# A 3x3 convolution: nine clipped taps in place of row pairs with a shared middle row

## The chip, the cores and the metric

The kernel runs on one core of a Trainium2 chip. The metric is the time of one execution on the device in microseconds; lower is better. Three runs of the kernel before took 132.85, 133.58 and 134.07 us, a median of 133.58.

## The reference

A 3x3 convolution with zero padding of one pixel, 16 images of 64 channels and 64x64 pixels, 128 output channels, all in f32:

```python
x:      (16, 64, 64, 64)   f32
weight: (128, 64, 3, 3)    f32
x_pad = np.pad(x, ((0, 0), (0, 0), (1, 1), (1, 1)), mode='constant')
for b, co, ci, kh, kw:
    output[b, co] += weight[co, ci, kh, kw] * x_pad[b, ci, kh:kh+h, kw:kw+w]
```

The output is (16, 128, 64, 64) in f32, 33.55 MB; the input x is 16.78 MB.

## The kernel before

**Loading.** Two images make a pair `p` (8 pairs): the 64 channels of one lie on partitions 0 to 63, those of the other on 64 to 127. Each pair has its own tile `xs` of 128 x 64 x 64 in f16, resident for the whole kernel. GpSimd's queue issues the loads (line 48), which cast f32 to f16 on the way: four pieces for pair 0 (rows 0-17, 18-31, 32-47, 48-63) and two for each other pair, eighteen in all, at the head of the program. The first piece holds every row that block 0 reads. SyncE's queue loads the weights (line 41) and later issues the stores.

**Weights.** ScalarE and VectorE cast the raw weights to f16, one kernel row `kh` at a time, and write each tap's 64 channels twice side by side (`w16`, lines 66 and 68). Nine transposes on TensorE (line 80) put them, channels on partitions, into PSUM, and as each was doubled the taps lie on both halves of the partitions. From PSUM five weight rows of three taps each are made in `Wt` (lines 86 to 90): G0, G1, G2 are the kernel's rows 0, 1, 2; G21 is row 2 minus row 1, G01 is row 0 minus row 1.

**The shared middle row.** Output rows are made in pairs 2j and 2j+1. With s[j] = x[2j] + x[2j+1], and U the convolution of s with the middle kernel row G1,

- output row 2j is U + G21 on x[2j+1] + G0 on x[2j-1],
- output row 2j+1 is U + G01 on x[2j] + G2 on x[2j+2].

That is five kernel rows of three taps for two output rows, where the direct form has six. The sums `ss` come from line 100: on VectorE in four pieces for pair 0, on GpSimd in two pieces for each other pair (one tile per pair, three tiles in rotation), kept in program order, so that GpSimd runs them behind the loads that it has to issue.

**Blocks.** Each pair has four blocks of 16 output rows (8 row pairs). A block has three groups of matmuls (line 137): U with 3 taps on `ss`; A with 6 taps for the even rows; B with 6 taps for the odd rows. A group has one PSUM tile of 128 x 8 x 64 for each of the two images. For a tap the two images' matmuls follow each other: one uses partitions 0 to 63 of weights and pixels, the other 64 to 127, so both halves of the array's rows are in use at once. Taps at the left and right column (kw 0 and 2) run over 63 columns, at the upper and lower image edge over 7 rows: no padded copy exists. A block is 3 x 2 + 6 x 2 + 6 x 2 = 30 matmuls of up to 512 columns.

**Evacuation.** ScalarE copies U's two tiles to SBUF (`ut`, line 151); VectorE adds A and U into the even rows of an output tile `ot` (line 156), B and U into its odd rows (line 159); SyncE stores each image's 16 rows, 512 KB (line 160). PSUM has eight tiles in rotation, `ot` sixteen, `ut` four. Waits between engines and the rotation of tiles are set by the framework from the program's order.

Of the kernel before, what the change touches and what calls it, by code (L numbers as in the profile page):

```python
# [8 lines left out]
F32 = mybir.dt.float32  # L9
F16 = mybir.dt.float16  # L10


@with_exitstack
def kernel(
    ctx: ExitStack,
    tc: tile.TileContext,
    x: bass.AP,
    weight: bass.AP,
    out: bass.AP,
):  # L20
    nc = tc.nc
    B, CI, H, W = x.shape
    CO = weight.shape[0]
    assert H == 64 and W == 64 and CI == 64 and CO == 128 and B % 2 == 0
    NP = B // 2
    RB = 8

    x_rows = x.rearrange("b c h w -> (b c) h w")
    out_rows = out.rearrange("b co h w -> b co h w")
    w_flat = weight.rearrange("co ci kh kw -> co (ci kh kw)")  # L30

    const = ctx.enter_context(tc.tile_pool(name="const", bufs=1))
    psum = ctx.enter_context(tc.tile_pool(name="psum", bufs=8, space=bass.MemoryType.PSUM))
    xpool = ctx.enter_context(tc.tile_pool(name="xpool", bufs=1))
    opool = ctx.enter_context(tc.tile_pool(name="opool", bufs=16))
    spool = ctx.enter_context(tc.tile_pool(name="spool", bufs=3))
    upool = ctx.enter_context(tc.tile_pool(name="upool", bufs=4))


    w_raw = const.tile([CO, CI, 9], F32)  # L40
    nc.sync.dma_start(w_raw.rearrange("p c t -> p (c t)"), w_flat)
    xs = []
    ident = const.tile([128, 128], F16)
    for p in range(NP):
        xt = xpool.tile([128, H, W], F16, tag=f"xs{p}", name="xs")
        cuts = [0, 18, 32, 48, 64] if p == 0 else [0, 32, 64]
        for lo, hi in zip(cuts[:-1], cuts[1:]):
            nc.gpsimd.dma_start(  # L48
                xt[:, lo:hi, :], x_rows[128 * p : 128 * p + 128, lo:hi, :]
            )  # L50
            if p == 0 and lo == 0:
                make_identity(nc, ident)
        xs.append(xt)


    w16 = const.tile([CO, 9, 2, CI], F16)
    for kh in range(3):
        src = (
            w_raw[:, :, 3 * kh : 3 * kh + 3]
            .rearrange("p c t -> p t c")  # L60
            .unsqueeze(2)
            .to_broadcast([CO, 3, 2, CI])
        )
        dst = w16[:, 3 * kh : 3 * kh + 3, :, :]
        if kh == 1:
            nc.vector.tensor_copy(dst, src)  # L66
        else:
            nc.scalar.copy(dst, src)  # L68

    Wt = const.tile([128, 5, 3, CO], F16)  # L70
    G0, G21, G1, G01, G2 = range(5)

    def wrow(i):
        return Wt[:, i, :, :].rearrange("p t c -> p (t c)")

    wps = {}
    for kh in (1, 0, 2):
        wp = psum.tile([128, 512], F32, tag="acc", name="wp")
        for k in range(3):
            nc.tensor.matmul(  # L80
                wp[:, k * CO : k * CO + CO],
                w16[:, 3 * kh + k, :, :].rearrange("p d c -> p (d c)"),
                ident,
            )
        wps[kh] = wp[:, 0 : 3 * CO]
    nc.vector.tensor_copy(wrow(G1), wps[1])  # L86
    nc.scalar.copy(wrow(G0), wps[0])  # L87
    nc.vector.tensor_sub(wrow(G21), wps[2], wrow(G1))  # L88
    nc.vector.tensor_sub(wrow(G01), wps[0], wrow(G1))  # L89
    nc.scalar.copy(wrow(G2), wps[2])  # L90


    ss = []
    for p in range(NP):
        st = spool.tile([128, H // 2, W], F16, tag="ss", name="ss")
        v = xs[p].rearrange("p (j i) c -> p j i c", i=2)
        step = 8 if p == 0 else 16
        for lo in range(0, H // 2, step):
            eng = nc.vector if p == 0 else nc.gpsimd
            add = eng.tensor_add(  # L100
                st[:, lo : lo + step, :], v[:, lo : lo + step, 0, :], v[:, lo : lo + step, 1, :]
            )
            if p > 0:
                tc.keep_in_program_order(add)
        ss.append(st)

        for blk in range(4):
            j0 = blk * RB

            def group(wi_rows):  # L110

                tiles = [
                    psum.tile([128, RB, W], F32, tag="acc", name="acc") for _ in range(2)
                ]
                n = 3 * len(wi_rows)
                i = 0
                for wi, off in wi_rows:
                    for kw in (1, 0, 2):
                        c_lo, c_hi = max(0, 1 - kw), min(W, W + 1 - kw)
                        for b2 in range(2):  # L120
                            p0 = 64 * b2
                            lo, hi = j0, j0 + RB
                            if off is None:
                                rhs = ss[p][p0 : p0 + 64, lo:hi, c_lo + kw - 1 : c_hi + kw - 1]
                            else:
                                while 2 * lo + off < 0:
                                    lo += 1
                                while 2 * (hi - 1) + off > H - 1:
                                    hi -= 1
                                first = 2 * lo + off  # L130
                                last = 2 * (hi - 1) + off
                                rhs = xs[p][
                                    p0 : p0 + 64,
                                    first : last + 1 : 2,
                                    c_lo + kw - 1 : c_hi + kw - 1,
                                ]
                            nc.tensor.matmul(  # L137
                                tiles[b2][:, lo - j0 : hi - j0, c_lo:c_hi],
                                Wt[p0 : p0 + 64, wi, kw, :],
                                rhs,  # L140
                                start=i == 0,
                                stop=i == n - 1,
                            )
                        i += 1
                return tiles

            U = group([(G1, None)])
            us = []
            for b2 in range(2):
                ut = upool.tile([128, RB, W], F32, tag="ut", name="ut")  # L150
                nc.scalar.copy(ut, U[b2])  # L151
                us.append(ut)
            ots = [opool.tile([128, RB, 2, W], F32, tag="ot", name="ot") for _ in range(2)]
            A = group([(G21, 1), (G0, -1)])
            for b2 in range(2):
                nc.vector.tensor_add(ots[b2][:, :, 0, :], A[b2], us[b2])  # L156
            Bt = group([(G01, 0), (G2, 2)])
            for b2 in range(2):
                nc.vector.tensor_add(ots[b2][:, :, 1, :], Bt[b2], us[b2])  # L159
                nc.sync.dma_start(  # L160
                    out_rows[2 * p + b2, :, blk * 16 : blk * 16 + 16, :],
                    ots[b2].rearrange("p j i c -> p (j i) c"),
                )


# [28 lines left out]
```

## Time and profile before

| | |
|---|---|
| median of three runs | 133.58 us |
| the profiled execution | 133.58 us, its span 131.8 us |
| TensorE matmul / weight load busy | 109.0 us (83%) / 53.5 us |
| VectorE busy | 84.5 us (64%) |
| ScalarE busy | 38.2 us (29%) |
| GpSimd busy | 39.6 us (30%) |
| mean granted TensorE clock | 0.956 |
| loads (software queue) | 8.39 MB written, 32.8% of the DMA engines' span |
| stores and weights (hardware queue) | 33.85 MB, 64.4% |
| HBM | 17.07 MB read, 33.55 MB written |

The span runs from the first to the last instruction of the profiled execution; the time of the execution has a little around it. A matmul's busy time is pipelined: neighbours overlap, so the sum of durations exceeds the busy time, and the pace has to be read from the starts. In a line of the groups stand the source line, the engine, the operation, what is written from what, the shapes and count; behind the first bar the busy time in us and the mean of one in ns; behind the second the engine's idle time just before them and what ended it. A line of the timeline has start and duration in us, engine, operation and how many are merged in it; in brackets the idle time before and its releaser.

### The profile page before, as it was taken

To read this page: it belongs to the slowest core of one execution; us is meant where nothing else is said; L and a number is where in the kernel's file an instruction comes from. 1 tells how busy PE (TensorE), PEld (TensorE's weight loads), DVE (VectorE), ACT (ScalarE), POOL (GpSimd) and SP (SyncE) were. 2 spreads that over 40 slices of the span, in tenths; PEclk is the share of its full clock that TensorE was granted. 3 is DMA by queue.
4 is the path that set the end of the run, shared out by engine and by line. 5 is a ranking of instruction groups with operands and counts; after the bars stand their busy time and mean duration, and the time that the engine had idled before them with its cause. 6 is when DMAs were issued, how large, how long until landed. Compare 5 with 4: busy or idle time off the path is not lost.

```text
span 131.8 us, 2482 instructions
## 1 busy us (share of the span) xinstructions
PE 109.0 (83%) x969; PEld 53.5 (41%) x969; DVE 84.5 (64%) x136; ACT 38.2 (29%) x69; POOL 39.6 (30%) x38
## 2 busy tenths in 40 slices
PE   0329999400899999999999999999999999999910
PEld 0203444200344555445554545554455544555400
DVE  0263777700057778777877777777778777877750
ACT  3604233000303333333333333333333333333300
POOL 6832131016999293009201910290000000000000
PEclk9999999975579999999999999999999999999997
DMA  3899999999999999999999999999999999888884
GB/s 97 115 185 208 211 216 280 285 280 277 277 277 271 277 278 285 276 302 411 421 420 419 410 418 418 419 415 416 418 419 411 421 404 369 348 351 332 334 332 159
DMA packets 11963, 42.39 MB, mean 322 GB/s; under 512 B 1328, under 2 KB 1456, under 8 KB 11952
## 3 DMA queue, kind: packets, MB, share of 16 engines
q1 hardware_dynamic: 9360, 33.85, 64.4%
q0 software_dynamic: 2592, 8.39, 32.8%
q8 instruction: 7, 0.11, 0.3%
q14 instruction: 4, 0.03, 0.1%
HBM read 17.07 MB, written 33.55 MB: 384 GB/s over the span
## 4 chain that ended last, share of the span: by engine, by line
PE 66%; DMA 21%; issue 4%; POOL 2%; DVE 1%; ACTq 1%; DVEq 0%; ACT 0%; POOLq 0%
PE acc L137 66%; DMA xs<-in_x_dram 21%; POOL ss L100 2%; ACTq L189 1%; DVE ot L156 1%; POOL xs L48 0%; DVEq L189 0%; DVE ot L159 0%; POOL ident masks.py:197 0%; ACT ut L151 0%; POOLq L178 0%
## 5 line engine op out<-in xcount | busy, mean ns | idle before, releaser
L137 PE MATMUL acc<-xs,Wt 64*128 64x504 f16 (+3 forms) x768 | 90.9, 385 | 0.0
L137 PEld LDWEIGHTS <-Wt 64*128 64x128 f16 x960 | 52.7, 97 | 66.9 <-issue 14.6
L156 DVE TENSOR_TENSOR ot<-acc,ut 128x512 f32<-128x512 f32 x64 | 41.2, 686 | 33.5 <-PE acc L137 17.1
L151 ACT COPY ut<-acc 128x512 f32<-128x512 f32 x64 | 34.4, 589 | 79.6 <-issue 75.3
L159 DVE TENSOR_TENSOR ot<-acc,ut 128x512 f32<-128x512 f32 x64 | 41.2, 685 | 1.1 <-PE acc L137 1.1
L100 POOL TENSOR_TENSOR ss<-xs 128x1024 f16<-128x1024 f16 x14 | 29.3, 2121 | 28.4 <-issue 28.4
L137 PE MATMUL acc<-ss,Wt 64*128 64x504 f16 (+1 forms) x192 | 27.6, 392 | 12.1 <-POOL ss L100 8.8
L48 POOL DMA_DIRECT2D xs<-in_x_dram x18 | 9.7, 547 | 20.7 <-DMA xs<-in_x_dram 19.9
L80 PE MATMUL wp<-ident,w 128*128 128x128 f16 x9 | 1.3, 306 | 4.5 <-DVE w L66 4.5
L100 DVE TENSOR_TENSOR ss<-xs 128x512 f16<-128x512 f16 x4 | 1.7, 423 | 4.1 <-DMA xs<-in_x_dram 4.1
L66 DVE CAST w<-w_raw 128x384 f16<-128x384 f32 x1 | 0.8, 836 | 3.6 <-DMA w_raw<-in_weight_dram 3.6
L80 PEld LDWEIGHTS <-w 128*128 128x128 f16 x9 | 0.8, 132 | 4.8 <-DVE w L66 4.5
L68 ACT CAST w<-w_raw 128x384 f16<-128x384 f32 x2 | 1.7, 873 | 1.6 <-DMA w_raw<-in_weight_dram 1.6
L90 ACT CAST Wt<-wp 128x384 f16<-128x384 f32 x1 | 0.5, 478 | 3.9 <-DVE Wt L88 3.9
L68 ACT ACT_TABLE_LOAD x1 | 1.3, 1283 | 0.7 <-PEq L178 0.7
L88 DVE TENSOR_TENSOR Wt<-wp,Wt 128x384 f16<-128x384 f32 x1 | 0.6, 559 | 0.1
L86 DVE CAST Wt<-wp 128x384 f16<-128x384 f32 x1 | 0.6, 551 | 0.0
L89 DVE TENSOR_TENSOR Wt<-wp,Wt 128x384 f16<-128x384 f32 x1 | 0.5, 548 | 0.0
L87 ACT CAST Wt<-wp 128x384 f16<-128x384 f32 x1 | 0.5, 478 | 0.1
masks.py:199 POOL TENSOR_SCALAR_AFFINE_SELECT ident<-ident 128x128 f16<-128x128 f16 x1 | 0.3, 304 | 0.1
masks.py:197 POOL MEMSET ident<- 128x128 f16 x1 | 0.2, 223 | 0.0
L178 POOL MEMSET const-float32-0.0<- 128x1 f32 x1 | 0.1, 98 | 0.2 <-issue 0.2
(3 smaller groups left out, 0.3 us busy)
## 6 DMA issues: line engine op xcount, KB each, us to landing
out_dram<-ot SPq DMA_DIRECT2D x64, 512.0 KB, 10.1
xs<-in_x_dram POOLq DMA_DIRECT2D x14, 512.0 KB, 25.5
xs<-in_x_dram POOLq DMA_DIRECT2D x2, 256.0 KB, 7.2
w_raw<-in_weight_dram SPq DMA_DIRECT2D x1, 288.0 KB, 2.9
xs<-in_x_dram POOLq DMA_DIRECT2D x1, 288.0 KB, 5.7
xs<-in_x_dram POOLq DMA_DIRECT2D x1, 224.0 KB, 6.1
```

The lines of the kernel that those rows point to most:

```text
L48: nc.gpsimd.dma_start(xt[:, lo:hi, :], x_rows[128 * p : 128 * p + 128, lo:hi, :])
L66: nc.vector.tensor_copy(dst, src)
L68: nc.scalar.copy(dst, src)
L80: nc.tensor.matmul(wp[:, k * CO : k * CO + CO], w16[:, 3 * kh + k, :, :].rearrange("p d c -> p (d c)"), ident,)
L86: nc.vector.tensor_copy(wrow(G1), wps[1])
L88: nc.vector.tensor_sub(wrow(G21), wps[2], wrow(G1))
L100: add = eng.tensor_add(st[:, lo : lo + step, :], v[:, lo : lo + step, 0, :], v[:, lo : lo + step, 1, :])
L137: nc.tensor.matmul(tiles[b2][:, lo - j0 : hi - j0, c_lo:c_hi], Wt[p0 : p0 + 64, wi, kw, :], rhs, start=i == 0, stop=i == n - 1,)
L151: nc.scalar.copy(ut, U[b2])
L156: nc.vector.tensor_add(ots[b2][:, :, 0, :], A[b2], us[b2])
L159: nc.vector.tensor_add(ots[b2][:, :, 1, :], Bt[b2], us[b2])
L189: with _tile.TileContext(nc) as tc:
```

## The change

The row sums, the five weight rows and the combination behind PSUM go. The nine taps' weights are copied from PSUM as they are (`Wt` of nine taps, three per copy, the middle row on VectorE, the others on ScalarE). A block of 16 output rows has four PSUM tiles: two halves of 8 rows for each of two images. For each of nine taps it has four matmuls, the halves outside and the images inside, and each reads the resident pixels directly, clipped to rows and columns that exist. Two tiles are copied to `ot` by VectorE (first image), two by ScalarE (second image), and SyncE stores 512 KB for each image as before. The loads (line 48), the casts and the transposes are not touched; the tiles `ss` and `ut` are no longer there.

```diff
-    spool = ctx.enter_context(tc.tile_pool(name="spool", bufs=3))
-    upool = ctx.enter_context(tc.tile_pool(name="upool", bufs=4))
...
-    Wt = const.tile([128, 5, 3, CO], F16)
...
+    Wt = const.tile([128, 9, CO], F16)
     for kh in (1, 0, 2):
         wp = psum.tile([128, 512], F32, tag="acc", name="wp")
...
-        wps[kh] = wp[:, 0 : 3 * CO]
-    nc.vector.tensor_copy(wrow(G1), wps[1])
-    nc.scalar.copy(wrow(G0), wps[0])
-    nc.vector.tensor_sub(wrow(G21), wps[2], wrow(G1))
-    nc.vector.tensor_sub(wrow(G01), wps[0], wrow(G1))
-    nc.scalar.copy(wrow(G2), wps[2])
+        dst = Wt[:, 3 * kh : 3 * kh + 3, :].rearrange("p t c -> p (t c)")
+        if kh == 1:
+            nc.vector.tensor_copy(dst, wp[:, 0 : 3 * CO])
+        else:
+            nc.scalar.copy(dst, wp[:, 0 : 3 * CO])
...
-            add = eng.tensor_add(
-                st[:, lo : lo + step, :], v[:, lo : lo + step, 0, :], v[:, lo : lo + step, 1, :]
-            )
...
-            U = group([(G1, None)])
...
-                nc.scalar.copy(ut, U[b2])
...
-            A = group([(G21, 1), (G0, -1)])
...
-                nc.vector.tensor_add(ots[b2][:, :, 0, :], A[b2], us[b2])
-            Bt = group([(G01, 0), (G2, 2)])
...
-                nc.vector.tensor_add(ots[b2][:, :, 1, :], Bt[b2], us[b2])
...
+    taps = [(1, 1), (1, 0), (1, 2), (0, 1), (0, 0), (0, 2), (2, 1), (2, 0), (2, 2)]
     for p in range(NP):
...
         for blk in range(4):
...
+            pst = [
+                psum.tile([128, RB, W], F32, tag="acc", name="acc") for _ in range(4)
+            ]
+            for ti, (kh, kw) in enumerate(taps):
+                c_lo, c_hi = max(0, 1 - kw), min(W, W + 1 - kw)
+                for rq in range(2):
+                    r0 = blk * 16 + rq * RB
+                    lo = max(r0, 1 - kh)
+                    hi = min(r0 + RB, H + 1 - kh)
+                    for b2 in range(2):
+                        p0 = 64 * b2
+                        nc.tensor.matmul(
+                            pst[2 * rq + b2][:, lo - r0 : hi - r0, c_lo:c_hi],
+                            Wt[p0 : p0 + 64, 3 * kh + kw, :],
+                            xs[p][
+                                p0 : p0 + 64,
+                                lo + kh - 1 : hi + kh - 1,
+                                c_lo + kw - 1 : c_hi + kw - 1,
+                            ],
+                            start=ti == 0,
+                            stop=ti == 8,
+                        )
             for b2 in range(2):
...
+                ot = opool.tile([128, 16, W], F32, tag="ot", name="ot")
+                for rq in range(2):
+                    src = pst[2 * rq + b2]
+                    dst = ot[:, rq * RB : rq * RB + RB, :]
+                    if b2 == 0:
+                        nc.vector.tensor_copy(dst, src)
+                    else:
+                        nc.scalar.copy(dst, src)
                 nc.sync.dma_start(
...
```

More of the change, by code (lines that the diff above doesn't have):

```diff
@@ L68 @@
             nc.scalar.copy(dst, src)
-    Wt = const.tile([128, 5, 3, CO], F16)
[L71 to L76, printed above, removed]
+    Wt = const.tile([128, 9, CO], F16)
     for kh in (1, 0, 2):
@@ L84 @@
             )
-        wps[kh] = wp[:, 0 : 3 * CO]
-    nc.vector.tensor_copy(wrow(G1), wps[1])
-    nc.scalar.copy(wrow(G0), wps[0])
-    nc.vector.tensor_sub(wrow(G21), wps[2], wrow(G1))
-    nc.vector.tensor_sub(wrow(G01), wps[0], wrow(G1))
-    nc.scalar.copy(wrow(G2), wps[2])
-    ss = []
-    for p in range(NP):
[L95 to L100, printed above, removed]
-                st[:, lo : lo + step, :], v[:, lo : lo + step, 0, :], v[:, lo : lo + step, 1, :]
-            )
-            if p > 0:
-                tc.keep_in_program_order(add)
-        ss.append(st)
-        for blk in range(4):
[L108 to L145, printed above, removed]
-            U = group([(G1, None)])
-            us = []
-            for b2 in range(2):
[L150 to L153, printed above, removed]
-            A = group([(G21, 1), (G0, -1)])
-            for b2 in range(2):
-                nc.vector.tensor_add(ots[b2][:, :, 0, :], A[b2], us[b2])
-            Bt = group([(G01, 0), (G2, 2)])
-            for b2 in range(2):
-                nc.vector.tensor_add(ots[b2][:, :, 1, :], Bt[b2], us[b2])
@@ L160 @@
                 nc.sync.dma_start(
-                    out_rows[2 * p + b2, :, blk * 16 : blk * 16 + 16, :],
-                    ots[b2].rearrange("p j i c -> p (j i) c"),
+                    out_rows[2 * p + b2, :, blk * 16 : blk * 16 + 16, :], ot
                 )
```

## The prediction

> **What bounds the kernel now.** I read the slices of the page first, then the groups, then the timeline around the one hole, then the stages by window. The page's slices of 3.3 us:
>
> ```profile
> PE   0329999400899999999999999999999999999910
> PEclk9999999975579999999999999999999999999997
> GB/s 97 115 185 208 211 216 280 285 280 277 277 277 271 277 278 285 276 302 411 421 420 419 410 418 418 419 415 416 418 419 411 421 404 369 348 351 332 334 332 159
> ```
>
> TensorE is full from the fourth slice to the end, except for a hole at slices 8 to 10. The transfers move about 280 GB/s until slice 17, 418 until slice 32 and less behind it: a backlog that is gone before the end. The groups:
>
> ```profile
> L137 PE MATMUL acc<-xs,Wt 64*128 64x504 f16 (+3 forms) x768 | 90.9, 385 | 0.0
> L137 PEld LDWEIGHTS <-Wt 64*128 64x128 f16 x960 | 52.7, 97 | 66.9 <-issue 14.6
> L100 POOL TENSOR_TENSOR ss<-xs 128x1024 f16<-128x1024 f16 x14 | 29.3, 2121 | 28.4 <-issue 28.4
> L137 PE MATMUL acc<-ss,Wt 64*128 64x504 f16 (+1 forms) x192 | 27.6, 392 | 12.1 <-POOL ss L100 8.8
> ```
>
> 768 + 192 = 960 matmuls, 30 for each of 32 blocks (8 image pairs, 4 blocks each). Their means of 385 ns are pipelined latencies and no pace. The 8.8 us at the end of the last line are the hole; the timeline tells where:
>
> ```profile
> 6.95 0.42 DVE L100 TENSOR_TENSOR ss<-xs 128x512 f16<-128x512 f16 x1 [2.46 <-DMA xs<-in_x_dram]
> ...
> 9.14 1.46 PE L137 MATMUL acc<-ss,Wt 64*128 64x512 f16 x6 [3.28 <-DVE Wt L86]
> ...
> 21.98 2.68 PE L137 MATMUL acc<-xs,Wt 64*128 64x512 f16 x24
> ...
> 30.75 0.53 POOL L48 DMA_DIRECT2D xs<-in_x_dram  x1 [3.24 <-DMA xs<-in_x_dram]
> 31.29 10.40 POOL L100 TENSOR_TENSOR ss<-xs 128x1024 f16<-128x1024 f16 x5
> 33.46 1.46 PE L137 MATMUL acc<-ss,Wt 64*128 64x512 f16 x6 [8.81 <-POOL ss L100]
> ```
>
> TensorE ends pair 0 at 24.66 (21.98 + 2.68) and stands until 33.46. GpSimd must make the row sums of pair 1, but its queue first issues the eighteen loads, and ten of these wait for an earlier load to land; the last leaves at 30.75. Pair 1's pixels had landed by about 16.45, when the issue that waited for its second half went. The chain of waits agrees: TensorE for 87.5 us from 33.46, and before it that sum and the loads.
>
> The pace, from the same timeline: the 24 matmuls of consecutive blocks begin at
>
> ```profile
> 97.30 2.69 PE L137 MATMUL acc<-xs,Wt 64*128 64x512 f16 x24
> ...
> 100.46 2.69 PE L137 MATMUL acc<-xs,Wt 64*128 64x512 f16 x24
> ...
> 103.62 2.77 PE L137 MATMUL acc<-xs,Wt 64*128 64x512 f16 x24
> ...
> 106.86 2.77 PE L137 MATMUL acc<-xs,Wt 64*128 64x512 f16 x24
> ```
>
> so a block takes 3.16 to 3.24 us. Over eleven of them (starts from 87.65 to 122.91) the mean is 3.205 us: 107 ns a matmul, or, as two matmuls on opposite halves of the rows go together, 214 ns a pair; 216 in an inner block (3.24 / 15). After each idle start the pace is half; the weight loads show it pair by pair:
>
> ```profile
> 11.25 0.15 PEld L137 LDWEIGHTS <-Wt 64*128 64x128 f16 x2 [0.28 <-ACT ut L151]
> 11.68 0.15 PEld L137 LDWEIGHTS <-Wt 64*128 64x128 f16 x2 [0.28 <-issue]
> 12.05 0.15 PEld L137 LDWEIGHTS <-Wt 64*128 64x128 f16 x2 [0.22 <-issue]
> 12.43 0.15 PEld L137 LDWEIGHTS <-Wt 64*128 64x128 f16 x2 [0.22 <-issue]
> ```
>
> 0.43 us a pair, and 0.375 for the three pairs at the image edge, which have 7 rows instead of 8. Time follows columns: 0.052 us for 63 columns is 0.83 ns a column, and 0.83 x 507 is 0.42, nearly the whole pair. At full pace 216 ns against 427 leaves some 5 ns that don't scale (2 x 216 - 427).
>
> **The change part by part.** *Matmuls.* A block has 9 taps x 2 row halves x 2 images = 36 in place of 30, of the same widths (512 and 504 columns; six of them at an image edge have 7 rows, as before). The halves alternate as before, so three pairs more: 3 x 216 ns = 0.648, and 3.205 + 0.648 = 3.853 us a block, x 32 = 123.3 us against 102.6: **+20.7 us**, on the path. If the 5 ns vanished, 18 x 32 x 5 ns = 2.9 us less; nothing in the trace makes a pair of such width slower than 216 at full clock, so this is the lower end and the value its own upper one.
>
> The Trainium skill ("TensorE: Matmul & The Clock Gate", "Back-to-back issue gap") gives N/2.4 + 2.5 ns, which for 507 columns is an estimate of 213.6 ns where the trace has 214 to 216; by it the sum would be about 1 us lower. Its sentence that isolated gaps over-count, with some 131 ns a matmul sustained at N = 512, has no counterpart in these rows: 216 ns a pair is what two concurrent streams leave.
>
> *The row sums* (14 on GpSimd, 4 on VectorE) go, and with them the hole: 33.46 - 24.66 = **-8.8 us**. What is late next? Matmuls of pair 1 need only its pixels. At about 15.4 us a pair, pair 1 is wanted at 25, pair 2 at 40, pair 3 at 56; those loads were in by 16.5, 22.3 and 30.8 (GpSimd's issues that waited for them). The loads themselves (L48) are the same lines; GpSimd's queue already gave them out as early as earlier landings let it, so nothing is gained there. The restart at half pace goes too: from 33.46 to 125.60, where TensorE's work ends by the stages, are 92.14 us for 28 blocks, 2.4 more than 28 x 3.205. **-2.4 us**.
>
> *The start.* The first matmul stood until 9.14 for the copy of the middle weights, which VectorE ran behind two row sums. Without these the copy can follow its transposes (at 4.54, all done at 5.86) and end by 6.4; ScalarE's two copies of 0.48 end by 6.9. Then the first pixels are last, at 6.95: start 7.0, **-2.1 us**, at worst -1.5 (a copy begun after them). The first ramp stays: 9.14 to 24.66 is 15.52 for four blocks, 2.7 over 4 x 3.205. I take 2.55, between the two ramps seen. Lower end 1.3, if the transposes and the short gap behind them (4.54 to 7.0) count toward it at half rate; upper 3.4, the same distance the other way, rounded down.
>
> *Evacuation.* Six tiles a block become four, copied, two by VectorE and two by ScalarE. Bounds for VectorE's copy: 551 ns (L86, 384 wide) and 686 (the 512-wide add); ScalarE's is 589 (L151). 1.4 us at most per engine in a block of 3.85, and eight banks hold two blocks: hidden, even at twice the price.
>
> *The end.* 131.8 - 125.6 = 6.2 us from the last matmul to the end:
>
> ```profile
> 125.67 1.28 DVE L159 TENSOR_TENSOR ot<-acc,ut 128x512 f32<-128x512 f32 x2
> ```
>
> two operations of VectorE, then the last stores. Afterwards there are two copies each on two engines, then the same two stores of 512 KB: 6.2 kept, give or take 0.6 (one store issue).
>
> Sum: 7.0 + 123.3 + 2.55 + 6.2 = 139.05 us of span. The profiled execution took 133.58 with a span of 131.8, so 1.78 lie around it, and it is the median itself: **140.8 us**.
>
> **Transfers as cover.** The stages that hold the backlog:
>
> ```profile
> 40.00:56.00 16.00, 16.00 (x152) 8.14 (x150) 12.52 (x21) 5.32 (x11) 7.97 (x4) 1.00 1.05 278
> 64.00:104.00 40.00, 40.00 (x378) 20.30 (x376) 31.80 (x52) 13.02 (x25) 8.43 (x4) 1.00 1.03 417
> ```
>
> (the last three columns: clock, DMA share, GB/s written). Stores alone run at 417. Loads read two bytes for each one written (f32 to f16): with loads L and stores S, 2L + S = 417 and L + S = 278 give L = S = 139. All together 2 x 8.39 + 33.55 + 0.3 = 50.6 MB, 121 us at 417: less than TensorE's 123.3 + 2.55, so no bound.
>
> The skill ("DMA: Bandwidth & Descriptors", "Specifications") puts a core's HBM limit at about 358 GB/s; by it 50.6 MB would take an estimated 141 us and the transfers would bound, near 145 in all. The 417 held for 40 us says no for this core.
>
> **The rivals.** *The output buffers run out (slower still).* Stores get 139 GB/s until the loads end, near 59 us, while blocks come at 1.05 MB per 3.85 us. By 59.4 thirteen blocks (26 buffers) are made; with 16 buffers, ten must have landed. The first store was issued at 15.76 and the mixed rate stood from 20 on; issued at 14.6 now (start, one block mostly at half pace, copies), they flow from some 18.5 and have 5.7 MB, 10.8 buffers. It just fits, and the two blocks of banks give 2.5 us more. For it: the margin is under one buffer. Against: after the loads, stores gain three buffers per block. Short by two buffers, a whole block waits: +3.9, 144.7 us. Chance 0.09.
>
> *The repeated weights come free (not slower).* The two row halves use one weight slice in succession. If loading weights set the pace (two of 97 ns are 194 of a pair's 216) and the second load were cheaper, pairs would shorten. It decides below 206 ns a pair: 576 x 10.3 ns = 5.9 us bring 140.8 to 134.9; 201 ns give 132.2. Against it: pairs follow columns, and 960 loads for 960 matmuls say that each keeps its own. Chance 0.03, likeliest 134. That the change does nothing to loading, despite its words, is in the forecast already; were the hole kept by another wait, it would be 140.8 + 11.2 = 152, chance 0.02.
>
> **How the numbers follow.** The forecast, 0.86, spans 138.4 (part of the 5 ns and a short ramp) to 142.5 (start, ramp and end at their worst add 2.1, less that they hardly meet). The range goes to 143.6 into the buffer case. Under 1% from 133.58 (132.2 to 134.9) can't be told from no change; only the weights rival lands there or below: same 0.02, faster 0.01, slower 0.97.
>
> **What would show it.** 1152 matmuls with inner blocks of 3.85 to 3.89 us; first matmul at 7.0; no idle of TensorE over 0.5 us after; GpSimd with loads alone; TensorE's work ending near 132.9. A wait of the copies for a landed store near 55 to 62 would mean the buffers; pairs under 210 ns the weights; a start past 8 us that something else held the weights or pixels.

## The result and the profile after

The changed kernel took 140.63 us (median of four runs, 140.01 to 141.58) against 133.41 us for the kernel before, run beside it: a ratio of 1.055, 95% interval 1.046 to 1.063. It is slower by 5.5%. The forecast was 140.8 us. The profiled execution took 140.28 us with a span of 138.5 and a mean granted clock of 0.993 (0.956 before).

The slices of its page, 3.5 us each:

```profile
PE   0389999999999999999999999999999999999910
PEclk9999999999999999999999999999999999999997
GB/s 105 118 186 212 213 279 279 277 277 277 277 277 279 275 278 277 282 381 419 420 418 413 418 421 419 415 414 413 424 379 324 276 304 306 298 266 237 273 257 189
```

The hole is gone: TensorE works without a break from the third slice to the end, and the clock stays up. The transfers again show three stages, 278, 418, and then a last one that starts earlier and lies lower: from slice 30 on the stores wait for TensorE, which makes 1.05 MB in 3.85 us (272 GB/s).

Its groups of instructions:

```profile
L96 PE MATMUL acc<-xs,Wt 64*128 64x504 f16 (+3 forms) x1152 | 124.7, 377 | 1.7 <-DMA xs<-in_x_dram 1.7
L96 PEld LDWEIGHTS <-Wt 64*128 64x128 f16 x1152 | 63.4, 95 | 62.8 <-issue 3.2
L113 DVE COPY ot<-acc 128x512 f32<-128x512 f32 x64 | 41.3, 686 | 86.6 <-issue 56.3
L115 ACT COPY ot<-acc 128x512 f32<-128x512 f32 x64 | 34.3, 589 | 92.5 <-PE acc L96 48.1
L46 POOL DMA_DIRECT2D xs<-in_x_dram x18 | 9.7, 545 | 21.7 <-DMA xs<-in_x_dram 20.9
```

1152 matmuls, and the only idle time before them is 1.7 us for the first pixels; the 8.8 us that stood behind the row sums have no successor. GpSimd has loads alone. Both copying engines are idle for two thirds of the time. Each matmul still has a weight load of its own.

The blocks can be counted by VectorE's copies, which begin when a block's first tile is complete. From the timeline:

```profile
7.50 16.72 PE L96 MATMUL acc<-xs,Wt 64*128 64x512 f16 x142 [1.72 <-DMA xs<-in_x_dram]
...
12.63 1.29 DVE L113 COPY ot<-acc 128x512 f32<-128x512 f32 x2 [7.07 <-PE acc L96]
...
16.52 1.29 DVE L113 COPY ot<-acc 128x512 f32<-128x512 f32 x2 [2.60 <-PE acc L96]
...
132.10 1.29 DVE L113 COPY ot<-acc 128x512 f32<-128x512 f32 x2 [2.55 <-issue]
```

Block 0 takes 5.13 us (7.50 to 12.63), the other 31 take (132.10 - 12.63) / 31 = 3.854 us each, and 6.4 us follow. That is the whole span: 7.5 + 5.13 + 119.47 + 6.4 = 138.5. By the timeline of TensorE its last matmul ends at 132.2.

### The profile page after: what moved, and what is told of

It reads as the page before. It is cut to its first block, busy times and chain, and to the rows that moved or that the text cites. A ratio compares the mean times of both kernels' runs of the same rounds, so it can differ in the third digit from the quotient of the medians.

```text
span 138.5 us, 2732 instructions
## 1 busy us (share of the span) xinstructions
PE 126.0 (91%) x1161; PEld 64.2 (46%) x1161; DVE 42.6 (31%) x66; ACT 38.2 (28%) x69; POOL 10.3 (7%) x24
## 4 chain that ended last, share of the span: by engine, by line
PE 88%; DMA 5%; issue 2%; DVE 0%; DVEq 0%; POOLq 0%
PE acc L96 88%; DMA xs<-in_x_dram 5%; DVE ot L113 0%; DVEq L144 0%; POOLq L133 0%
## 5 line engine op out<-in xcount | busy, mean ns | idle before, releaser
L96 PE MATMUL acc<-xs,Wt 64*128 64x504 f16 (+3 forms) x1152 | 124.7, 377 | 1.7 <-DMA xs<-in_x_dram 1.7
L96 PEld LDWEIGHTS <-Wt 64*128 64x128 f16 x1152 | 63.4, 95 | 62.8 <-issue 3.2
L113 DVE COPY ot<-acc 128x512 f32<-128x512 f32 x64 | 41.3, 686 | 86.6 <-issue 56.3
L115 ACT COPY ot<-acc 128x512 f32<-128x512 f32 x64 | 34.3, 589 | 92.5 <-PE acc L96 48.1
```

The source lines that it names most:

```text
L96: nc.tensor.matmul(pst[2 * rq + b2][:, lo - r0 : hi - r0, c_lo:c_hi], Wt[p0 : p0 + 64, 3 * kh + kw, :], xs[p][p0 : p0 + 64, lo + kh - 1 : ...
```

## The experiments

Three questions were open. Is the price of the added matmuls really one of columns? What was the removed hole worth, in the kernel before and in the changed one? How near are the output buffers and the transfers to taking over?

**No row sums, 30 matmuls.** The kernel before without any wait for GpSimd; the middle-row group reads row 2j alone.

```diff
-        st = spool.tile([128, H // 2, W], F16, tag="ss", name="ss")
...
-                                rhs = ss[p][p0 : p0 + 64, lo:hi, c_lo + kw - 1 : c_hi + kw - 1]
+                                rhs = xs[p][
+                                    p0 : p0 + 64,
+                                    2 * lo : 2 * hi - 1 : 2,
+                                    c_lo + kw - 1 : c_hi + kw - 1,
+                                ]
```

> The kernel before with 30 matmuls a block, its row sums left out: the middle-row group reads the pixel row 2j alone, so the lower row's share in that group is missing from the output. No wait for GpSimd is left. Theory 'each removed wait is worth its length': the hole (8.8), its restart at half pace (2.4) and the later start (2.1) come off, 133.4 - 13.3 = 120.1 us. Rival 'transfers take over': loads and stores go side by side at 139 GB/s each until 59 us, then about 27.8 MB of stores are left, 66.6 us at 417 GB/s, ending near 126 and landing some 2.6 us later: span 128, time about 129.8 us, with TensorE waiting for free output buffers from about 50 us on.

131.76 us, a ratio of 0.994 (0.990 to 0.998) to the kernel before. Of the 13.3 us of waits that were taken away, 1.4 came off the time. Its page:

```profile
PE   0479999999999999439999999999999999995000
GB/s 100 145 179 211 205 266 276 278 275 276 275 283 279 279 270 280 276 274 372 420 419 410 418 419 420 412 415 420 419 414 418 415 420 413 419 419 413 422 323 13
```

Now the transfers run at some 418 GB/s to slice 38; nothing is left of the stage in which stores waited for TensorE. TensorE has a gap in slices 17 and 18 instead and is done at 118.7 us, 11 us before the end. Its waits name the gap:

```profile
DVE ot L146 <- DMA out_dram<-ot: 9.8, 5, 3.1
...
PE acc L127 <- DVE ot L146: 3.8, 2, 3.4
```

VectorE waited for stores to land and free an output buffer, and TensorE for VectorE. The transfers had taken over, as the rival said; at 131.8 it came 2 us later than reckoned from bytes.

**The sums on VectorE.** Again no wait for GpSimd behind the loads, but with the computation complete: VectorE makes all row sums.

```diff
-            eng = nc.vector if p == 0 else nc.gpsimd
-            add = eng.tensor_add(
...
+            add = nc.vector.tensor_add(
...
+            if p + 1 < NP:
+                sums(p + 1, [blk])
             Bt = group([(G01, 0), (G2, 2)])
```

> The kernel before, complete, with the row sums of all pairs on VectorE, a quarter of the next pair's after each block's even rows, instead of on GpSimd behind the loads. Theory 'each removed wait is worth its length': hole and restart come off, the start stays, 133.4 - 11.2 = 122.2 us. Rival 'transfers take over': about 130 us as without sums at all; a longer VectorE (some 12 us more work, 96 of 130 us) is no bound.

132.12 us, 0.995 (0.991 to 0.999): the hole's length is not to be had this way either, and again the time is 2 us above the rival's 130. TensorE ran without a gap to 55 us and then waited 3.4 us for VectorE, which waited for stores.

**The same with 24 output buffers.** Here the question was whether the buffers or the transfers hold it.

```diff
-    opool = ctx.enter_context(tc.tile_pool(name="opool", bufs=16))
+    opool = ctx.enter_context(tc.tile_pool(name="opool", bufs=24))
```

> The kernel with all row sums on VectorE (132.1 us), with 24 output buffers instead of 16. There TensorE waits some 4 us for output buffers near 57 us and again near 62. Theory 'the transfers set the end, the buffers only show it': TensorE's wait goes, its last matmul comes some 4 us earlier, and the time stays at 132.1 us within 1%, since the stores run at 417 GB/s to the end either way. Rival 'the wait for buffers is on the path': about 128 us.

132.28 us, 0.991 (0.987 to 0.994). Behind its start TensorE now waits for nothing and is done by some 114 us. The stages of its end (start to end and length, then busy time and count of TensorE, its weight loads, VectorE, ScalarE, GpSimd, then clock, DMA share, GB/s):

```profile
112.00:116.00 4.00, 1.65 (x16) 0.57 (x12) 2.48 (x4) 0.29 (x1) 0.00 (x0) 1.00 1.02 415
116.00:120.00 4.00, 0.00 (x0) 0.00 (x0) 0.00 (x0) 0.00 (x0) 0.00 (x0) 0.83 1.03 423
120.00:124.00 4.00, 0.00 (x0) 0.00 (x0) 0.00 (x0) 0.00 (x0) 0.00 (x0) 0.50 1.03 420
124.00:128.00 4.00, 0.00 (x0) 0.00 (x0) 0.00 (x0) 0.00 (x0) 0.00 (x0) 0.50 0.43 174
```

For ten microseconds no engine computes and the stores still run at 420 GB/s. With these loads and stores that is a floor of the transfers, near 132 us in all, which an earlier end of TensorE does not lower. The chain of waits of this run gives TensorE 76% of the span; it doesn't show the floor, because the chain leaves by the last instruction and not by the queue of stores.

**The hole put back into the changed kernel.** Pair 1 is read from a copy that GpSimd makes behind the loads.

```diff
+    held = xpool.tile([128, H, W], F16, tag="held", name="held")
+    for lo, hi in ((0, 18), (18, 32), (32, 48), (48, 64)):
+        cp = nc.gpsimd.tensor_copy(held[:, lo:hi, :], xs[1][:, lo:hi, :])
+        tc.keep_in_program_order(cp)
+    xs[1] = held
```

> The changed kernel, complete, with the old hole put back: pair 1 is read from a copy that GpSimd makes behind the eighteen loads in its queue. TensorE would end pair 0 at 24.2; the last load is issued at 31.7, and the first copied piece is there near 34.7 (0.5 for the issue, some 2.4 for 1152 elements by the 2.1 us that a row sum of 1024 took): a hole of 10.5 and a restart at half pace of 1.2 to 2.7. Theory 'here TensorE sets the end, so a hole costs its length': 140.6 + 10.5 + 2 = 153 us. Rival 'the transfers absorb the hole, as in the kernel before, where taking it away was worth 1.4 us': 142 us.

150.92 us, against 140.63 without: 10.3 us more. Its timeline for TensorE:

```profile
6.93 18.24 PE L102 MATMUL acc<-xs,Wt 64*128 64x512 f16 x144 [1.14 <-DMA xs<-in_x_dram]
32.88 17.23 PE L102 MATMUL acc<-held,Wt 64*128 64x512 f16 x144 [7.71 <-POOL held L84]
49.93 92.58 PE L102 MATMUL acc<-xs,Wt 64*128 64x512 f16 x864
```

There are 7.7 us of hole, and the 144 matmuls behind it take 17.23 us where four blocks of 3.854 take 15.42: a restart of 1.8. The hole was shorter than the 10.5 us expected for two reasons: the copies took 1 us a piece, less than half of what was reckoned, so that TensorE went on at 32.88 and not 34.7, and pair 0 ended at 25.2 and not at 24.2. Together hole and restart are 9.5 of the 10.3 us; the rest is the first block, which began 0.6 earlier here and lost 1.3 more at half pace (see the warm start). Here a hole costs its length and its restart. In the kernel before, removing it gave 1.4 us.

**Ten taps.** The middle tap is added twice.

```diff
-    taps = [(1, 1), (1, 0), (1, 2), (0, 1), (0, 0), (0, 2), (2, 1), (2, 0), (2, 2)]
+    taps = [(1, 1), (1, 0), (1, 2), (0, 1), (0, 0), (0, 2), (2, 1), (2, 0), (2, 2), (1, 1)]
...
-                            stop=ti == 8,
+                            stop=ti == 9,
```

> The changed kernel with a tenth tap: the middle tap (1,1) is added a second time, so its share of the output is doubled. 40 matmuls a block instead of 36. Theory 'columns set the pace': two more pairs of 512 columns a block, 2 x 216 ns x 32 = 13.8 us, 140.6 + 13.8 = 154.4 us. Rival 'weight loads set the pace, and a slice loaded twice in succession costs less': pairs of the same weights cost less than 216 ns, under 153 us. Rival 'transfers set the time': no change, 140.6 us.

154.63 us: 14.0 more than with nine taps, where 13.8 were expected. Copies of ScalarE in its timeline:

```profile
60.02 1.07 ACT L115 COPY ot<-acc 128x512 f32<-128x512 f32 x2 [3.17 <-PE acc L96]
...
98.56 1.07 ACT L115 COPY ot<-acc 128x512 f32<-128x512 f32 x2 [3.17 <-issue]
```

nine blocks in 38.54 us, 4.28 each, 0.43 over the 3.854 of nine taps: two pairs of 214 ns, though their weight slice is the same.

**Halves outside the taps.** No slice is loaded twice in succession.

```diff
-            for ti, (kh, kw) in enumerate(taps):
-                c_lo, c_hi = max(0, 1 - kw), min(W, W + 1 - kw)
-                for rq in range(2):
+            for rq in range(2):
+                for ti, (kh, kw) in enumerate(taps):
+                    c_lo, c_hi = max(0, 1 - kw), min(W, W + 1 - kw)
```

> The changed kernel with the two row halves outside the nine taps, so that no weight slice is loaded twice in succession; the same 36 matmuls. Theory 'columns set the pace': 140.6 us, within 1%. Rival 'repeated weights come cheaper': slower by over 1%, as the saving is lost.

139.84 us, a ratio of 1.052 (1.045 to 1.060) where the changed kernel has 1.055: no loss, so repeated slices brought none of the pace. The two experiments on weights agree. They add or reorder columns and weight loads together; which of the two sets the pace is told by the edge blocks, in the rows with 16 buffers below.

**Fewer output buffers.** One number of the changed kernel, 16, becomes 12 and then 14.

```diff
-    opool = ctx.enter_context(tc.tile_pool(name="opool", bufs=16))
+    opool = ctx.enter_context(tc.tile_pool(name="opool", bufs=12))
```

> The changed kernel with 12 output buffers instead of 16. Stores have 139 GB/s until the loads end near 60 us. By 55.5 us block 12's copies need 12 stores landed where some 10 are, by 59.4 block 13's need 14 where 11 are; two blocks of banks hide 2.5 us of each delay. Theory 'the backlog takes nearly sixteen buffers': a stall of about one block, 140.6 + 4 = 144.6 us (142.5 to 147). Rival 'buffers have no part in it': 140.6 us.

> The changed kernel with 14 output buffers instead of 16. Theory 'the backlog takes nearly sixteen': block 13's copies at 59.4 need 12 stores landed where 11 are; the delay of some 3 us is mostly hidden by the second block of banks, so 140.6 to 141.5 us, with copies that wait for a landed store near 60 us. Rival 'the margin is less than reckoned': 142 us or more.

145.3 us with 12, 140.87 with 14. VectorE's timeline, with 12:

```profile
53.83 1.29 DVE L113 COPY ot<-acc 128x512 f32<-128x512 f32 x2 [4.80 <-DMA out_dram<-ot]
61.37 1.29 DVE L113 COPY ot<-acc 128x512 f32<-128x512 f32 x2 [6.25 <-DMA out_dram<-ot]
64.34 1.29 DVE L113 COPY ot<-acc 128x512 f32<-128x512 f32 x2 [1.68 <-DMA out_dram<-ot]
```

with 14:

```profile
55.07 1.29 DVE L113 COPY ot<-acc 128x512 f32<-128x512 f32 x2 [2.54 <-PE acc L96]
60.60 1.29 DVE L113 COPY ot<-acc 128x512 f32<-128x512 f32 x2 [4.24 <-DMA out_dram<-ot]
63.68 1.29 DVE L113 COPY ot<-acc 128x512 f32<-128x512 f32 x2 [1.80 <-DMA out_dram<-ot]
```

and with 16:

```profile
55.10 1.29 DVE L113 COPY ot<-acc 128x512 f32<-128x512 f32 x2 [2.55 <-issue]
58.88 1.29 DVE L113 COPY ot<-acc 128x512 f32<-128x512 f32 x2 [2.49 <-issue]
62.77 1.29 DVE L113 COPY ot<-acc 128x512 f32<-128x512 f32 x2 [2.60 <-PE acc L96]
66.66 1.29 DVE L113 COPY ot<-acc 128x512 f32<-128x512 f32 x2 [2.60 <-PE acc L96]
70.50 1.29 DVE L113 COPY ot<-acc 128x512 f32<-128x512 f32 x2 [2.55 <-issue]
```

Sixteen keep the rhythm of 3.8 to 3.9 us through the stretch near 59 us. With 14 one interval is 5.5 us and the next 3.1: the banks absorb it, and TensorE has no gap. With 12, intervals reach 7.5, and the kernel loses 4.7 us: TensorE waits 2.4 us for a free PSUM tile, and loses some 2 more at half pace behind that wait (719 matmuls in 79.2 us, where 107 ns each make 77).

The rows with 16 also part columns from weight loads. They span the four blocks of one image pair, which take 3.78, 3.89, 3.89 and 3.84 us. The first and the last touch an image edge: three of their 18 pairs of matmuls have 7 rows instead of 8, 63 or 64 columns fewer, and as many weight loads. The two are 0.16 us shorter together, 27 ns for each of six pairs, and 63 of 507 columns at 216 ns are 27 ns too. (By the mean of 3.854 over all blocks it is 24.)

**A warm start.** Twelve matmuls on zeros fill TensorE's idle time ahead of the first block.

```diff
+    zt = const.tile([128, 512], F16)
+    nc.vector.memset(zt, 0.0)
+
+    def warm(n):
+        zp = psum.tile([128, 512], F32, tag="acc", name="zp")
+        for _ in range(n):
+            tc.keep_in_program_order(nc.tensor.matmul(zp, zt[:, 0:128], zt))
+
+    warm(8)
...
+    warm(4)
     taps = [(1, 1), (1, 0), (1, 2), (0, 1), (0, 0), (0, 2), (2, 1), (2, 0), (2, 2)]
```

> The changed kernel with twelve matmuls on a tile of zeros added while TensorE would be idle at the start, eight ahead of the transposes and four behind them. Theory 'the first block loses time to a half-pace start': the 1.2 us that block 0 took over 3.85 go, and with them the difference between executions (spans of 138.2 and 138.5 at a clock of 0.993, 139.2 and 139.8 at 0.985): near 139 us, clock 0.997 or more, block 0 in 3.9 us. Rival 'block 0 is slow for another reason, its pixels or its weights': no change, or up to 1 us slower if the added matmuls run past 7.5 us.

138.47 us, 1.040 (1.036 to 1.044) times the kernel before; the interval lies below that of the changed kernel. Its timeline:

```profile
5.57 1.64 PE L47 MATMUL zp<-zt 128*128 128x512 f16 x4
...
7.54 6.80 PE L106 MATMUL acc<-xs,Wt 64*128 64x512 f16 x62 [0.33 <-DMA xs<-in_x_dram]
...
11.32 1.29 DVE L123 COPY ot<-acc 128x512 f32<-128x512 f32 x2 [5.62 <-PE acc L106]
```

Block 0 takes 3.78 us, as a first block of a pair does at full pace (55.10 to 58.88 in the rows with 16 buffers), against 5.13: 1.35 us of half pace are gone. The added matmuls take the half pace on themselves: the last four stand 0.43 us apart, as the pairs of block 0 did in the changed kernel:

```profile
8.31 0.18 PEld L96 LDWEIGHTS <-Wt 64*128 64x128 f16 x2 [0.25 <-issue]
8.74 0.17 PEld L96 LDWEIGHTS <-Wt 64*128 64x128 f16 x2 [0.25 <-issue]
```

The expected clock of 0.997 was not reached (0.984 to 0.996), but that tells nothing of the start. The changed kernel's page gives 9 tenths or more in the slices where these rows lie, and what its mean of 0.993 lacks is all in the last slice, behind TensorE's work. With the warm start the page reads

```profile
PEclk9999999999999999999999999999999999999995
```

and its mean is 0.985 because the clock fell 2.2 us after the last matmul there, and 4.3 us after it in the changed kernel. Among the warm starts one of 138.03 us has 0.984, one of 138.65 has 0.996. The expectation read the difference in mean clock as a longer start; the traces don't bear that out.

Nor is the half pace of one length. Block 0 is the same code in the changed kernel, with 14 and with 12 buffers and with the hole put back, and began at 7.50, 7.22, 7.58 and 6.93 us; ScalarE's first copies, in this order and with the warm start last, where it began at 7.54:

```profile
12.66 1.07 ACT L115 COPY ot<-acc 128x512 f32<-128x512 f32 x2 [6.36 <-PE acc L96]
...
12.63 1.07 ACT L115 COPY ot<-acc 128x512 f32<-128x512 f32 x2 [6.27 <-PE acc L96]
...
13.03 1.07 ACT L115 COPY ot<-acc 128x512 f32<-128x512 f32 x2 [6.75 <-PE acc L96]
...
13.42 1.07 ACT L121 COPY ot<-acc 128x512 f32<-128x512 f32 x2 [7.12 <-PE acc L102]
...
11.36 1.07 ACT L125 COPY ot<-acc 128x512 f32<-128x512 f32 x2 [5.03 <-PE acc L106]
```

That is 5.16, 5.41, 5.45 and 6.49 us against 3.82: a ramp of 1.3 to 2.7 us from one execution to another.

## Why the prediction held, point by point

- **Matmuls, +20.7.** Forecast 3.853 us a block, measured 3.854. The edge blocks show that columns set it, 27 ns for 63 of them with the same number of weight loads; ten taps and halves outside show that a repeated slice is no cheaper. The rival of repeated weights fell in both.
- **The start.** Forecast 7.0, measured 7.50, on the first pixels as said; over the experiments on the changed kernel with the same loads the first matmul came between 6.75 and 7.58, so it is the spread of the first load's landing.
- **The ramp.** Forecast 2.55 us, measured 1.35 in the profiled execution: the term that was furthest off, at the lower end of 1.3 that was given. It is not one number: executions with the same first block have 1.3 to 2.7, so that 2.55 lay within what this kernel does, and one profile could not size it. (Its upper end was mis-reckoned: the same distance the other way is 3.8, not 3.4.) That the transposes had already counted, or where in some period the start fell, was not told apart. A spread of this size would account for most of that between the four executions (spans of 138.2 to 139.8), but only one of these was profiled. The Trainium skill ("TensorE: Matmul & The Clock Gate", "What's actually happening") has the clock follow a free-running window, so that the ramp depends on where in it the first matmul falls; a ramp of 1.3 to 2.7 us agrees in kind, but no run here shows the window itself.
- **The end.** Forecast 6.2 from the last matmul, measured 6.3 (132.2 to 138.5).
- **The sum.** Start 0.5 too early, ramp 1.2 too long, end 0.1 too short: 139.05 of span forecast, 138.5 measured. That 140.8 came within 0.2 us of the median is in part luck, since two errors partly cancel and the four executions spread over 1.6 us; that it came within one per cent is not, since the matmuls are nine tenths of it and were right.
- **Evacuation and loads.** Hidden, as said; both engines idle most of the time, no wait for pixels after the first; nothing took the hole's place.
- **The buffers.** "It just fits" was right: 16 leave no wait, 14 a wait that is hidden, 12 cost 4.7 us, where the expectation put 4 and the prediction 3.9 for being two buffers short. Two buffers fewer still cost nothing, so the one buffer of margin and the banks' 2.5 us were together enough for two.
- **What bounded the kernel before.** Here the reading was right in the sum and wrong in what it implies. TensorE with its hole did set 133 us, but the transfers stood 1.4 us behind, at 131.8, not at the 126 or so that 121 us of bytes and a short landing suggest. Listing the hole as -8.8 and the restart as -2.4 was legitimate only because the added matmuls keep TensorE above that floor. By itself, the removal is worth 1.1 to 1.4 us; the experiments without the sums, with the sums elsewhere and with more buffers all end there. Seen from the floor, the change adds about 8.9 us (140.6 - 131.8); by these runs it could hardly have gained more than 1.4 with the same loads and stores, however cheap its matmuls.

A complete version that beats both kernels is the one with all sums on VectorE, at 132.1 to 132.3 us: 0.5 to 0.9% under the kernel before, and no more, since the transfers end it. Whether the last 4 to 5 us between the end of the bulk of the stores and the end of the span can be shortened was not tried.

## What to carry to other kernels

Before a wait is priced at its length, work out where the next limit stands with that wait gone: a stage of transfers at their full rate whose backlog drains shortly before the end means that nearly all of the gain will be taken back. Waits of 11 to 13 us were worth 1.1 to 1.4 under one limit, and a hole of 7.7 with its restart cost 9.5 under another. When the array is the limit and two half-height matmuls already share it, count columns: using a weight slice twice in succession brings nothing, and a fifth more matmuls cost a fifth more of the array's time. And size a start at half pace from several executions, or fill it.

## What the runs showed of the hardware

The half pace at the start can be filled: twelve matmuls on zeros, in time that TensorE would have idled, took 2.2 us off the median and 1.3 off the span of the profiled execution. The page's granted clock doesn't show it: it reads full while pairs stand 0.43 us apart at the start, though in the kernel before, at the restart behind the hole, it reads 0.50 at the same spacing. A load that converts f32 to f16 weighs about twice what it writes: from 24 to 56 us of the changed kernel, the loads write 4.44 MB in 68.4% of the DMA engines' time and the stores 4.41 MB in 36.5%, 139 and 138 GB/s side by side, where stores alone make 417. And the floor of the transfers lies later than bytes alone say: 50.6 MB at 417 GB/s are 121 us, yet with the transfers never short of work the spans were 129.8 and 130.6. Part of it is the slow start (100, 145 and 179 GB/s in the first three slices of the kernel without sums), part the last slice of 3.2 us, in which next to nothing moves (13 GB/s).
